# Making the triangular inverses of two DeltaNet heads together instead of one at a time

## The chip, the cores and the metric

The kernel runs on one core of one Trainium2 chip. The metric is device time of the whole program in microseconds (us). Before the change three runs took 2318.16, 2314.65 and 2317.48 us, a median of 2317.48 us. PE is the matrix engine (PEld its weight load), DVE, ACT and POOL are the vector, scalar and GpSimd engines, and SP is the queue that issues every DMA of this kernel.

## The reference, cut to what matters

One hybrid encoder layer over 2048 prompt positions and a 32-position sample, width 1024, all in 32-bit floats. A combined input projection feeds a spatial-gating mixer and a gated DeltaNet with 4 heads of 128; an output projection and a feed-forward of width 4096 follow. The change is inside the DeltaNet. For every head and chunk the reference solves a unit triangular system:

```
kb = k * beta[..., None]
a = jnp.einsum('bhnid,bhnjd->bhnij', kb, k) * dec_strict
lmat = a + jnp.eye(C, dtype=a.dtype)
rhs = jnp.concatenate([v * beta[..., None], kb * jnp.exp(gc)[..., None]], axis=-1)
sol = lax.linalg.triangular_solve(lmat, rhs, left_side=True, lower=True, unit_diagonal=True)
...
def step(s, inp):
    v_new = u_i - jnp.einsum('bhck,bhkv->bhcv', w_i, s)
    o = jnp.einsum('bhck,bhkv->bhcv', qg_i, s) + jnp.einsum('bhij,bhjv->bhiv', attn_i, v_new)
    s = s * gl_i[..., None, None] + jnp.einsum('bhck,bhcv->bhkv', kg_i, v_new)
```

The kernel works in chunks of 128 positions and forms the inverse of each 128x128 unit triangular matrix itself. There are 16 such chunks per head, in two halves of the sequence with 8 chunks each, and a small 32-position one for the sample.

## The kernel before, in words

The program records operations, each with an engine, an estimated duration, its operands and a priority, and a list scheduler (`schedule`, line 249) then writes them out in one order per engine. Each engine executes its list strictly in that order. Six priorities exist: CHAIN (the recurrence), INV (the inverses), LOCAL, EVAC, GEMM (the large projections) and IDLE. PE's list is mostly large matmuls of 260 to 512 columns (tiles `g`, `f`), with small bursts put between them when the scheduler's clock says that their operands are ready. On PE, `schedule` adds to an operation's cost 95 or 110 ns when the array's tile shape changes, and 84 ns (`TURN`) when a large matmul follows a small one.

The stages are: start-up; per half of the sequence `v_stage`, the q/k/v projections, the DeltaNet parts and `u_stage`; then `out_stage` for each half; then the feed-forward. The DeltaNet of one head and half has three parts.

- `delta_local` (LOCAL) forms, per pair of chunks, the decayed key products; they land in a buffer `nb` of 8 matrices of 128x128 (tile `M` of `delta_inv`).
- `delta_inv` (INV, line 1236) inverts the 8 matrices. The 16x16 diagonal blocks go by DMA to a layout with one block per partition (64 rows of 256 numbers), and `solve` (line 1298) inverts them on POOL with 15 pairs of multiply and subtract. They go back by DMA into `ud`. PE then doubles the size of the inverted blocks: from 16 to 32 with two bursts of 32 matmuls each on four 32x32 quarters of the array (`pa`, `pb`), from 32 to 64 with two bursts on 32x32 places (`p1` on two places, 16 matmuls; `p2` on three, 24 matmuls, the third making a transpose), and from 64 to 128 with two bursts of 8 matmuls on one 64x64 quarter (`p3`, `p4`). Each result is negated or copied by DVE before the next burst reads it. All use the one PSUM bank `B`.
- `delta_chain` (CHAIN, line 1411) runs over the chunks for heads 0 and 1 together, then 2 and 3, and needs both heads' inverses. Each chunk has three small bursts in banks `C`.

A 32-bit matmul of such a burst is two instructions in the trace, so 32 calls are 64 instructions there. `sample` does the same for the 32 sample positions, with its own solve on 8 rows. The chain's and the sample's outputs go through DRAM (`mix_d`) and are read back by `load_group` (line 943) into `BH`/`BL` for `out_stage`. The staging tiles of `load_group`, `x_stats`, `v_tile` and `gate_tile` come from the ring `E`, with six places of 512 columns before.

## Time and profile before

| what | value |
|---|---|
| median of the runs shown | 2317.48 us (2314.65 to 2318.16) |
| span of the profiled execution, first to last instruction | 2313.1 us |
| what the median has beyond that span | 4.4 us |
| PE busy | 2289.8 us, 99% |
| DVE, ACT, POOL busy | 1664.5, 1228.2, 602.1 us |

The page gives the profiled execution's own time as its span; the 4.4 us beside it are the difference to the median of other executions. Timeline rows give the start in us from the first instruction, the time from the first start to the last end of a merged group, the engine, the source line, the operation, the tiles (`out<-in`), the shapes and the number of instructions. `32*32 32x16` is a matmul on 32 rows and 32 columns of the array with 16 moving columns. Matmuls overlap in the pipeline, so what a group costs PE is read from the starts of the large matmuls on either side of it, not from its own length.

### The profile page before, as it was taken

To read this page: it belongs to the slowest core of one execution; us is meant where nothing else is said; L and a number is where in the kernel's file an instruction comes from. 1 tells how busy PE (TensorE), PEld (TensorE's weight loads), DVE (VectorE), ACT (ScalarE), POOL (GpSimd) and SP (SyncE) were. 2 spreads that over 40 slices of the span, in tenths; PEclk is the share of its full clock that TensorE was granted. 3 is DMA by queue.
4 is the path that set the end of the run, shared out by engine and by line. 5 is a ranking of instruction groups with operands and counts; after the bars stand their busy time and mean duration, and the time that the engine had idled before them with its cause. 6 is when DMAs were issued, how large, how long until landed. Compare 5 with 4: busy or idle time off the path is not lost.

```text
span 2313.1 us, 45814 instructions
## 1 busy us (share of the span) xinstructions
PE 2289.8 (99%) x16018; PEld 2178.3 (94%) x16018; DVE 1664.5 (72%) x3619; ACT 1228.2 (53%) x2809; POOL 602.1 (26%) x846
## 2 busy tenths in 40 slices
PE   9999999999999999999999999999999999999998
PEld 6887779999999988999999999999999999999998
DVE  6657656677654555589999999876668886666775
ACT  4665657566564434476555545753344564344344
POOL 1224443324333023444445424210000250000001
PEclk9999999999999999999999999999999999999999
DMA  8478876666566766887777787997667797766771
GB/s 314 147 253 297 258 227 221 186 203 209 169 200 187 244 203 217 265 295 256 257 252 262 254 282 241 336 327 237 216 215 257 257 305 231 223 215 217 250 223 54
DMA packets 358327, 547.08 MB, mean 237 GB/s; under 512 B 66424, under 2 KB 182284, under 8 KB 358096
## 3 DMA queue, kind: packets, MB, share of 16 engines
q1 hardware_dynamic: 358096, 544.16, 72.5%
q8 instruction: 126, 2.06, 0.4%
q14 instruction: 105, 0.86, 0.1%
HBM read 390.96 MB, written 153.05 MB: 235 GB/s over the span
## 4 chain that ended last, share of the span: by engine, by line
PE 65%; DVE 2%; DMA 1%; issue 1%; ACT 1%; POOL 0%; POOLq 0%; DVEq 0%; SPq 0%; ACTq 0%
PE f L416 53%; PE g L416 10%; PE C L416 1%; DMA s<-th_d 1%; DVE s L370 1%; POOL s L370 0%; DVE wl L370 0%; ACT s L355 0%; PE B L416 0%; DVE BL L370 0%; DMA x_d<-s 0%; PE C L427 0%; PE M L416 0%; PE M L427 0%; ACT BH L355 0%
## 5 line engine op out<-in xcount | busy, mean ns | idle before, releaser
L355 ACT ACTIVATE s<-s 128x348 f32<-128x348 f32 (+12 forms) x1067 | 490.7, 484 | 328.7 <-DVE s L370 144.4
L416 PE MATMUL f<-s,wh 128*128 128x348 f32 (+1 forms) x2768 | 662.0, 322 | 0.5 <-DVE s L370 0.3
L416 PEld LDWEIGHTS f<-s,wh 128*128 128x128 f32 x2768 | 481.0, 188 | 1.8 <-DVE s L370 1.4
L370 DVE TENSOR_TENSOR s<-f,s 128x348 f32<-128x348 f32 (+1 forms) x696 | 347.4, 511 | 168.2 <-PE f L416 167.5
L416 PE MATMUL f<-s,wl 128*128 128x348 f32 (+1 forms) x1384 | 444.7, 321 | 0.0
L416 PE MATMUL g<-BH,wh 128*128 128x384 f32 (+2 forms) x1088 | 399.5, 367 | 3.4 <-ACT BH L355 3.4
L416 PE MATMUL g<-BH,wl 128*128 128x384 f32 (+2 forms) x1088 | 382.3, 351 | 0.0
L416 PE MATMUL g<-BL,wh 128*128 128x384 f32 (+2 forms) x1088 | 381.2, 350 | 0.3 <-DVE BL L375 0.3
L370 DVE TENSOR_TENSOR s<-s,s 128x348 fp32r<-128x348 f32 (+8 forms) x674 | 347.1, 544 | 40.7 <-ACT s L355 16.9
L416 PE MATMUL f<-BL,wh 128*128 128x348 f32 (+1 forms) x1024 | 330.1, 322 | 0.0
L416 PE MATMUL f<-BH,wh 128*128 128x348 f32 (+1 forms) x1024 | 329.0, 321 | 0.0
L416 PE MATMUL f<-BH,wl 128*128 128x348 f32 (+1 forms) x1024 | 328.6, 321 | 0.0
L355 ACT ACTIVATE wh<-s 128x512 fp32r<-128x512 f32 x282 | 176.4, 632 | 234.7 <-PE f L416 178.7
L370 POOL TENSOR_TENSOR s<-s 64x15 f32<-64x15 f32 (+12 forms) x328 | 163.9, 500 | 447.3 <-issue 382.1
L370 POOL TENSOR_TENSOR s<-s,s 128x512 f32<-128x512 f32 (+5 forms) x153 | 186.3, 1225 | 308.2 <-ACT s L355 155.5
L416 PEld LDWEIGHTS f<-s,wl 128*128 128x128 f32 x1384 | 260.5, 188 | 0.0
L370 DVE TENSOR_TENSOR wl<-s,wh 128x512 fp32r<-128x512 f32 x282 | 221.4, 792 | 37.1 <-ACT wh L355 36.6
L416 PEld LDWEIGHTS g<-BH,wh 128*128 128x128 f32 x1088 | 205.0, 188 | 26.6 <-issue 4.9
L416 PEld LDWEIGHTS g<-BL,wh 128*128 128x128 f32 x1088 | 205.5, 189 | 17.2 <-DVE BL L375 0.9
L416 PEld LDWEIGHTS g<-BH,wl 128*128 128x128 f32 x1088 | 204.6, 188 | 18.2
L375 DVE SCALAR_TENSOR_TENSOR s<-s,s,s 128x256 f32<-128x256 f32 (+4 forms) x314 | 163.9, 547 | 53.7 <-ACT s L355 29.1
L416 PEld LDWEIGHTS f<-BH,wl 128*128 128x128 f32 x1024 | 192.6, 188 | 0.0
(133 smaller groups left out, 3350.0 us busy)
## 6 DMA issues: line engine op xcount, KB each, us to landing
s<-w_u SPq DMA_DIRECT2D x124, 256.0 KB, 4.0
s<-w_d SPq DMA_DIRECT2D x121, 256.0 KB, 3.4
wh<-su_d SPq DMA_DIRECT2D x114, 256.0 KB, 3.8
wl<-su_d SPq DMA_DIRECT2D x114, 256.0 KB, 3.9
wh<-sd_d SPq DMA_DIRECT2D x100, 256.0 KB, 3.1
wl<-sd_d SPq DMA_DIRECT2D x100, 256.0 KB, 3.9
wr<-w_b SPq DMA_DIRECT2D x36, 512.0 KB, 5.1
s<-adaw SPq DMA_DIRECT2D x32, 512.0 KB, 6.1
```

The costliest lines, as they stand in the source:

```text
L355: self.p.op(ACT, c, lambda: nc.scalar.activation(out=R(out), in_=R(in_), func=func, **{k: R(v) for k, v in kw.items()}), [out, accum], [in ...
L370: self.p.op(eng, c, lambda: e.tensor_tensor(out=R(out), in0=R(a), in1=R(b), op=op), [out], [a, b])
L375: self.p.op(DVE, c, lambda: nc.vector.scalar_tensor_tensor(out=R(out), in0=R(a), scalar=R(s), in1=R(b), op0=op0, op1=op1), [out], [a, s, b])
L416: nc.tensor.matmul(R(out), R(l), R(r), **kw)
```

## The change

The inverses are made for a pair of heads at once. `delta` now collects two `nb` buffers and calls `delta_inv` once for both. `solve` works on 128 rows instead of 64. Each burst of 16, 32 and 64 covers 16 chunks. The third place of `p2` is gone: the transpose that it made is now a DVE 32x32-block transpose. The step from 64 to 128 has three bursts instead of four for two heads: the upward products of the first head; then the downward products of the first head and the upward ones of the second, alternating, on two different quarters of the array; then the downward ones of the second. The scheduler no longer adds anything for a changed tile shape or for a turn to a large matmul, and the bursts have other durations in it. To make room, `nb` has three places instead of two, the ring `E` four instead of six, and `N`, `U`, `tmp`, `ud`, `td`, `z0`, `z1` lie elsewhere.

```diff
-TURN = 84
...
             if e == PE:
-                if o.table and o.table != grid:
-                    end += 110 if o.table == (P, P) else 95
-                    grid = o.table
-                elif o.prio == GEMM and not large:
-                    end += TURN
                 large = o.prio == GEMM
...
-        rg("nb", [(5, 0), (24, 0)], (P, 1024))
+        rg("nb", [(5, 0), (24, 0), (23, 0)], (P, 1024))
...
-        rg("E", hv(21, 22, 23), (P, 512))
+        rg("E", hv(21, 22), (P, 512))
...
-        with self.p.at(INV):
-            self.delta_inv(hf, h, nb)
+        self.nbs.append(nb)
+        if len(self.nbs) == 2:
+            with self.p.at(INV):
+                self.delta_inv(hf, h // 2, self.nbs)
+            self.nbs = []
...
-        Uv = self.solve(64, nd)
+        Uv = self.solve(128, nd)
...
-        at = [(c, a, slice(32 * a, 32 * a + 32)) for c in range(8) for a in range(4)]
+        C = range(16)
+        at = [(c, a, slice(32 * a, 32 * a + 32)) for c in C for a in range(4)]
-        self.mms([(pa[x, 16 * c : 16 * c + 16], M[x, c, x], td[x, c, 0:16], kw(32 * a, 32 * a)) for c, a, x in at], 480)
+        self.mms([(pa[x, 16 * c : 16 * c + 16], M(x, c, x), td[x, c, 0:16], kw(32 * a, 32 * a)) for c, a, x in at], 1396)
...
-        self.mms([(p1[hi[p], 32 * e : 32 * e + 32], M[lo[p], e, hi[p]], td[lo[p], e], kw(64 * p, 64 * p + 32))
-                  for e in range(8) for p in range(2)], 350)
+        self.mms([(p1[hi[p], 32 * c : 32 * c + 32], M(lo[p], c, hi[p]), td[lo[p], c], kw(64 * p, 64 * p + 32))
+                  for c in C for p in range(2)], 800)
...
-            calls.append((p2[32:64, 256 + 32 * e : 288 + 32 * e], ud[32:64, e], z1[32:64, e], kw(32, 32)))
-        self.mms(calls, 380)
-        self.cp(TA[32:64, :, 0:32], e8(p2[32:64, 256:512]))
+        self.mms([(p2[lo[p], 32 * c : 32 * c + 32], z1[hi[p], c], ud[hi[p], c], kw(64 * p + 32, 64 * p))
+                  for c in C for p in range(2)], 800)
+        self.transpose32(TA[32:64, :, 0:32], bl(p2[0:32, 0:512], 32))
...
-        self.mms([(p3[64:128, 64 * e : 64 * e + 64], M[0:64, e, 64:128], TA[:, e], kw(0, 64)) for e in range(8)], 880)
-        self.ts(z2[64:128], e8(p3[64:128, 0:512]), -1.0, ALU.mult)
-        p4 = self.bank("B")
-        self.mms([(p4[0:64, 64 * e : 64 * e + 64], z2[64:128, e], M[64:128, e, 64:128], kw(64, 0)) for e in range(8)], 880)
+        up = lambda c: (p3[64:128, 64 * (c % 8) : 64 * (c % 8) + 64], M(slice(0, 64), c, slice(64, 128)), TA[:, c], kw(0, 64))
+        dn = lambda c: (p3[0:64, 64 * (c % 8) : 64 * (c % 8) + 64], z2[64:128, c], M(slice(64, 128), c, slice(64, 128)), kw(64, 0))
+        self.mms([up(c) for c in range(8)], 1251)
+        self.ts(z2[64:128, heads[0]], bl(p3[64:128, 0:512], 64), -1.0, ALU.mult)
+        self.mms([f for c in range(8) for f in (dn(c), up(c + 8))], 1251)
+        self.ts(z2[64:128, heads[1]], bl(p3[64:128, 0:512], 64), -1.0, ALU.mult)
+        self.cp(Ms[0][0:64, :, 64:128], bl(p3[0:64, 0:512], 64))
+        self.dma(self.us_d[2 * pair][hf], nbs[0])
+        self.mms([dn(c) for c in range(8, 16)], 1251)
```

Where the instructions stand. The first place is PE's list at the step from 64 to 128 of the last head (before) and of the last two heads (after) of the second half. `B_...` is the PSUM bank of the inverses, `g_...` a bank of a large projection, `C_...` a bank of the chain; `s_...` are slots of SBUF. Before:

```order
L416 MATMUL g_9278<-BH_74,wl 128x384
L416 MATMUL B_9388<-s_477,s_491 64x64 x8
L416 MATMUL g_9278<-BH_75,wh 128x384
...
L416 MATMUL g_9278<-BH_78,wl 128x384
L416 MATMUL B_9427<-s_491,s_477 64x64 x8
L427 MATMUL C_9312<-ident,s_471 128x128 x2
```

and now:

```order
L410 MATMUL C_9255<-s_477,s_465 128x128 x4
L410 MATMUL B_9250<-s_473,s_468 64x64 x8
L410 MATMUL g_9140<-BH_77,wh 128x288
...
L410 MATMUL g_9241<-BH_75,wl 128x288
L410 MATMUL B_9250<-s_468,s_473 64x64
L410 MATMUL B_9250<-s_473,s_487 64x64
...
L410 MATMUL g_9241<-BH_76,wh 128x288
...
L410 MATMUL g_9307<-BH_74,wl 128x288
L410 MATMUL B_9250<-s_487,s_473 64x64 x8
```

Two bursts of 8 per head became three for two heads; the middle one alternates single matmuls whose weights are `s_468` and `s_473`, 16 in all. All three write the same bank.

The second place is PE's list at the end of the sample's chain: its last transpose (`C_...<-ident`), and behind it the first large matmul of `out_stage` for the second half (the first `128x384` after the `128x512`) and the first one that reads the sample's columns (`128x288`). Before:

```order
L416 MATMUL g_10486<-BH_73,wl 128x512
L427 MATMUL C_10469<-ident,s_473 128x128
L416 MATMUL g_10486<-BH_74,wh 128x512
...
L416 MATMUL g_10624<-BH_71,wh 128x384
...
L416 MATMUL g_10827<-BH_71,wh 128x288
```

and now:

```order
L410 MATMUL g_10303<-BH_71,wh 128x384
...
L410 MATMUL g_10404<-BH_75,wl 128x384
L421 MATMUL C_10375<-ident,s_469 128x128
L410 MATMUL M_10379<-ones,s_487 128x1 x4
L410 MATMUL g_10404<-BH_76,wh 128x384
...
L410 MATMUL g_10549<-BH_71,wh 128x288
```

Between the transpose and the first matmul on the sample's columns stood 159 large matmuls, and now stand 57: the transpose, with the chain ahead of it, has moved back by 102 large matmuls.

## The prediction

> **What bounds the kernel now.** I read the page first, then the busy times by stage, then PE's timeline around the bursts of the inverses. The page:

> ```profile
> span 2313.1 us, 45814 instructions
> PE 2289.8 (99%) x16018; PEld 2178.3 (94%) x16018; DVE 1664.5 (72%) x3619; ACT 1228.2 (53%) x2809; POOL 602.1 (26%) x846
> ```

> PE is idle for 23 us of 2313. The inverses lie between 300 and 770 us; the busy times of the two stretches that hold them (length; PE, PEld, DVE, ACT, POOL; clock; DMA) say the same of that place alone:

> ```profile
> 230.00:480.00 250.00, 247.88 (x2339) 216.67 (x2338) 161.25 (x490) 154.55 (x457) 91.13 (x199) 1.00 0.72 223
> 600.00:780.00 180.00, 179.39 (x1844) 172.14 (x1844) 102.29 (x318) 93.05 (x270) 64.30 (x178) 1.00 0.63 190
> ```

> There PE idles 2.1 of 250 us and 0.6 of 180 us, at full granted clock. So what an inverse does on DVE, ACT, POOL or by DMA is covered by large matmuls, and the time is PE's list added up. The change is worth what it takes from that list, less the new places where PE has to stand.

> **What a burst costs now.** In PE's timeline I take the start of the large matmul before a burst and of the second one after it, and subtract two ordinary pitches between large matmuls. Counting to the second one includes what the first pays to get back in.

> ```profile
> 635.84 0.29 PE L416 MATMUL g<-BH,wh 128*128 128x288 f32 x1
> 635.97 0.29 PE L416 MATMUL g<-BL,wh 128*128 128x288 f32 x1
> 636.10 0.29 PE L416 MATMUL g<-BH,wl 128*128 128x288 f32 x1
> 636.33 0.73 PE L416 MATMUL B<-s,s 32*32 32x16 f32 x64
> 636.98 0.40 PE L416 MATMUL g<-BH,wh 128*128 128x288 f32 x1
> 637.22 0.29 PE L416 MATMUL g<-BL,wh 128*128 128x288 f32 x1
> ...
> 596.40 0.29 PE L416 MATMUL g<-BH,wl 128*128 128x288 f32 x1
> 596.62 0.69 PE L416 MATMUL B<-s,s 32*32 32x32 f32 x32
> 597.24 0.40 PE L416 MATMUL g<-BH,wh 128*128 128x288 f32 x1
> 597.48 0.29 PE L416 MATMUL g<-BL,wh 128*128 128x288 f32 x1
> ...
> 470.54 0.34 PE L416 MATMUL g<-BL,wh 128*128 128x384 f32 x1
> 470.72 0.34 PE L416 MATMUL g<-BH,wl 128*128 128x384 f32 x1
> 470.99 0.70 PE L416 MATMUL B<-s,s 32*32 32x32 f32 x48
> 471.62 0.44 PE L416 MATMUL g<-BH,wh 128*128 128x384 f32 x1
> 471.89 0.33 PE L416 MATMUL g<-BL,wh 128*128 128x384 f32 x1
> ...
> 760.46 0.33 PE L416 MATMUL g<-BH,wl 128*128 128x384 f32 x1
> 760.72 1.14 PE L416 MATMUL B<-s,s 64*64 64x64 f32 x16
> 761.79 0.45 PE L416 MATMUL g<-BH,wh 128*128 128x384 f32 x1
> 762.08 0.34 PE L416 MATMUL g<-BL,wh 128*128 128x384 f32 x1
> ```

> The pitch is 0.13 us at 288 columns (635.84, 635.97, 636.10) and 0.18 at 384 (470.54, 470.72). A burst of 16 costs 637.22 - 636.10 - 0.26 = 0.86 us, the first burst of 32 costs 597.48 - 596.40 - 0.26 = 0.82, the second 471.89 - 470.72 - 0.36 = 0.81, a burst of 64 costs 762.08 - 760.46 - 0.36 = 1.26. A head has two, one, one and two of them: 1.72 + 0.82 + 0.81 + 2.52 = 5.87 us, and the 8 heads (4 in each half) 47.0 us.

> The same rows show what a burst is made of. The groups by form give the length of one instruction (number, busy us, mean ns, idle time before them):

> ```profile
> L416 PE MATMUL B<-s,s 64*64 64x64 f32 x256 | 18.2, 221 | 0.2 <-DVE s L393 0.2
> L416 PE MATMUL B<-s,s 32*32 32x16 f32 x1032 | 12.0, 180 | 0.4 <-DVE s L401 0.4
> L416 PE MATMUL B<-s,s 32*32 32x32 f32 x640 | 11.2, 192 | 0.0
> ```

> Bursts of 32, 48 and 64 instructions of the 32x32 forms last 0.69, 0.70 and 0.73 us, nearly the same, because they use two, three and four places of the array and each place gets 16. Less one instruction (0.19 or 0.18) that is 0.50, 0.51 and 0.55 us, or 0.031 to 0.034 us for a round in which every place takes one instruction. So different places run beside each other at no cost, all writing one PSUM bank. On a single 64x64 place the round takes (1.14 - 0.22) / 15 = 0.061 us. What is left of a burst's price, 0.86 - 0.55 = 0.31 or 0.82 - 0.50 = 0.32 us, is paid once per burst for entering and leaving.

> **The change part by part.** *Joint small bursts.* A joint burst has 32 rounds on each place where a single one had 16. It costs one more set of rounds and saves one entry: 0.86 + 0.55 = 1.41 for 16, 0.82 + 0.50 = 1.32 and 0.81 + 0.50 = 1.31 for 32 (the third place that p2 loses ran beside the others, so dropping it gives nothing). For a pair of heads 2 x 1.41 + 1.32 + 1.31 = 5.45 us, in place of 2 x 3.35 = 6.70: 1.25 saved.

> *The step of 64.* The outer bursts stay at 1.26. The middle one has 32 instructions on two quarters, with different rows and different columns. If they run beside each other as the 32x32 places do, it takes 16 rounds and half a round more: 1.26 + 0.03 = 1.29. If not, 16 further instructions at 0.061 come on top: 1.26 + 0.98 = 2.24. I take 1.29, since the nearest rows (two places with different rows and columns, 0.69 us for 32 instructions) behave so. Then a pair costs 1.26 + 1.29 + 1.26 = 3.81 in place of 5.04: 1.23 saved; with no overlap 0.28.

> *Sum.* 1.25 + 1.23 = 2.48 us per pair of heads; there are 4 pairs (two per half), so 9.9 us. Against the profiled span 2313.1 - 9.9 = 2303.2 us; the median of the runs has 4.4 us beyond that span, so 2307.6 us. With no overlap the saving is 4 x 1.53 = 6.1 us.

> *POOL.* A solve of 64 rows and the sample's of 8 rows, 30 instructions each:

> ```profile
> 671.83 11.43 POOL L370 TENSOR_TENSOR s<-s 64x15 f32<-64x15 f32 x30 [6.84 <-DMA s<-nd_d]
> 742.46 11.99 POOL L370 TENSOR_TENSOR s<-s 8x15 f32<-8x15 f32 x30 [5.00 <-DMA s<-nds_d]
> ```

> Eight rows take as long as 64, so 128 should too, and four solves (46 us) leave POOL. I count that at nothing: PE does not wait for POOL in this stretch. The smaller count of copies, table loads and DMAs is counted at nothing for the same reason; the large matmuls cover it.

> *The scheduler's durations.* No charge is left for a turn to large matmuls. PE's order stays a fixed list; a charge only moves a burst forward or back in it. Now 800 ns stand for bursts of 32 that cost about 1.3 us by the sum above. The scheduler's PE is then ahead of the real one, so more large matmuls than needed stand before the next step, which makes a wait on PE rarer. I count it at nothing.

> *The end of the chain.* The inverse of heads 2 and 3 now waits for both, and with it their chain and the sample's last transpose, which moves from the row at 888.68 to the place of the row at 912.47, 57 large matmuls before the row at 922.98. Its outputs must go to DRAM and back and be split before that.

> ```profile
> 888.68 0.27 PE L427 MATMUL C<-ident,s 128*128 128x128 f32 x1
> ...
> 912.47 0.34 PE L416 MATMUL g<-BH,wh 128*128 128x384 f32 x1
> ...
> 922.98 0.30 PE L416 MATMUL g<-BH,wh 128*128 128x288 f32 x1
> ...
> 888.99 0.35 DVE L375 SCALAR_TENSOR_TENSOR s<-C,s,s 128x128 f32<-128x128 f32 x1 [1.45 <-PE C L427]
> ...
> DMA to landing us min/median/max: 1.5/3.9/6.1
> ...
> 914.88 0.46 DVE L370 TENSOR_TENSOR BL<-s,BH 128x288 fp32r<-128x288 f32 x1 [0.29 <-ACT BH L355]
> ```

> The path is 0.31 + 0.35 to the end of the DVE step, two landings on mix_d of 3.9 at the median, and about 0.9 for the two halves of the split (0.46 each): 9.4 us, against 10.5. At the longest landings (6.1) it is 13.8, and PE would stand some 3 us, with the loads behind it in SP's queue late by as much. I take none and keep 3 for the range. The ring E with four places instead of six hits the same loads: a wave of four takes a landing and a split, about 5 us, so the 8 tiles of a group take 10 us, while 48 large matmuls at 0.18 us, 8.6 us, stand between two groups in PE's list. Two groups short by 1.4 us give 0 to 3 us more.

> [...]

> **The rivals.** [...]

> *New waits eat part of it*: the late end of the chain and the four places of E, 2 to 6 us together. For it: the margin of 1.1 us above. Against it: the short waits of today. It gives 2309.6 to 2313.6, in the middle 2311.6 us. This is also the case in which the pairs do not pay as meant, because an inverse that waits for two heads is later.

> *The chain's steps come too late in PE's list*: slower. The other durations reshuffle all dependent bursts, and where PE arrives before the operand it stands, with every large matmul queued behind. There are 96 chain bursts (2 halves x 2 pairs x 8 chunks x 3) and 28 of the inverses. It decides from a mean wait of 0.12 us on each of the 124 on: 14.9 us, 2307.6 + 14.9 = 2322.5 us. Today's waits speak against it, 0.6 and 0.4 us in total:

> ```profile
> PE C L416 <- ACT s L355: 0.6, 1, 0.6
> PE B L416 <- DVE s L401: 0.4, 1, 0.4
> ```

> *More than the sum*: two of today's waits of PE on ACT between large matmuls, 3.1 us, could happen to vanish with fewer table loads. It gives 2304.5 us.

> **How the numbers follow.** The full sum, with waits within 2 us of today's, has 0.57; no overlap 0.10; new waits 0.20; late chain steps 0.07; more than the sum 0.06. The predicted time is that of the first, 2307.6 us. The range reaches down to 2303.5, a little below the last case, and up to 2314.5, past the first three cases; it leaves out the late chain steps and the ends of the others. I call a change of over 0.2% (4.6 us, so below 2312.8 or above 2322.1) one that a measurement of this kernel can tell. Faster then has nearly all of the first, second and last cases and about half of the third, lowered for what a reshuffled list can hide: 0.79. Within 0.2% gets 0.14 and slower 0.07.

> **What would show it.** In the changed kernel's timeline a burst of 128 instructions of the form 32x16 should last about 1.28 us, one of 64 of the form 32x32 about 1.2, and the middle burst of 32 of the form 64x64 about 1.17 us; 2.1 us there means no overlap. PE's busy time should fall by some 9 us with its idle time near 23 us. POOL should fall by about 46 us, and a solve should stay near 11 to 12 us. The prediction is wrong if PE's idle time grows by more than 3 us; the places to look are the chain's bursts after 700 us and the loads of mix_d before 923 us.

## The result, and the profile after

The changed kernel takes 2321.86 us (median of 6 runs, 2320.62 to 2328.52), the kernel before took 2317.14 us beside it (6 runs, 2314.62 to 2318.16). The ratio is 1.0031 with a 95% interval of 1.0021 to 1.0041: slower, by about 7 us by the ratio (the two medians differ by 4.7 us), where 9.9 us of gain were forecast. The profiled execution has a span of 2320.9 us (before 2313.1).

The page of the changed kernel, span and engine line:

```profile
span 2320.9 us, 45340 instructions
PE 2289.5 (99%) x15890; PEld 2180.3 (94%) x15890; DVE 1651.0 (71%) x3591; ACT 1215.4 (52%) x2794; POOL 568.1 (24%) x722
```

POOL fell by 34 us, but PE's busy time did not fall. The same two stretches as in the prediction, with the columns named there:

```profile
230.00:480.00 250.00, 243.32 (x2144) 215.87 (x2144) 150.83 (x443) 146.34 (x435) 77.96 (x142) 0.97 0.69 215
600.00:780.00 180.00, 177.38 (x1883) 172.65 (x1882) 96.13 (x303) 90.13 (x270) 55.32 (x151) 0.99 0.62 186
```

PE now idles 6.7 us of the first stretch (before 2.1) and 2.6 us of the second (before 0.6), and the granted clock, 1.00 before, is 0.97 and 0.99. What PE waits for (total us, times, longest):

```profile
PE B L410 <- issue: 6.7, 4, 2.2
PE f L410 <- DVE s L364: 2.7, 4, 1.1
PE C L410 <- DMA s<-us_d: 2.3, 1, 2.3
```

The first line is new. "Issue" means that PE stood although nothing that the profile shows held it. PE's timeline around the first pair's two joint steps of 16 shows where:

```profile
340.22 0.40 PE L410 MATMUL g<-BH,wl 128*128 128x512 f32 x1
340.54 1.26 PE L410 MATMUL B<-s,s 32*32 32x16 f32 x128
...
344.19 0.61 PE L410 MATMUL B<-s,s 32*32 32x16 f32 x50
346.97 0.84 PE L410 MATMUL B<-s,s 32*32 32x16 f32 x78 [2.17 <-issue]
```

The first joint burst lasts 1.26 us (1.28 was forecast). The second one stops after 50 of its 128 matmuls for 2.17 us, in the middle of a list of calls that are all ready. All four pairs do so; the other three stops are 1.92, 1.80 and 0.82 us long.

The next view is the busy time, the granted clock and the DMA share in four short stretches behind such stops (columns as above):

```profile
348.76:352.17 3.41, 3.41 (x10) 2.65 (x9) 0.28 (x1) 3.37 (x10) 0.00 (x0) 0.50 0.23 39
386.31:389.72 3.41, 3.41 (x18) 3.41 (x17) 3.26 (x12) 2.94 (x7) 0.00 (x0) 0.50 0.47 155
464.81:471.64 6.83, 6.83 (x26) 6.54 (x25) 3.13 (x8) 4.35 (x12) 0.00 (x0) 0.50 0.42 118
645.72:649.13 3.41, 3.41 (x62) 3.01 (x62) 2.08 (x6) 1.51 (x6) 0.18 (x1) 0.50 0.12 41
```

PE counts as busy through all 17.06 us of them, at half the clock. About half of that time is lost (8.5 us by the clock, 7.9 us against the median pitch of the same forms), and no line of waits shows it. In the kernel before, the trace has no such stretch between 20 and 2300 us. Three of the four follow the stops of 1.80 to 2.17 us in the bursts. The one at 386.31 follows a wait of the first pair's chain for the inverse's output:

```profile
383.15 0.38 PE L410 MATMUL C<-s,s 128*128 128x128 f32 x2
385.88 0.49 PE L410 MATMUL C<-s,s 128*128 128x128 f32 x2 [2.35 <-DMA s<-us_d]
386.12 0.41 PE L410 MATMUL g<-wh,BH 128*128 128x260 f32 x1
386.33 0.42 PE L410 MATMUL g<-wl,BH 128*128 128x260 f32 x1
```

The pitch of the large matmuls of 260 columns behind it is 0.21 us (386.12 to 386.33); a few us earlier, between 378 and 381 us, it is 0.12 us.

The bursts that do not stop cost what was forecast. The timeline shows the middle step of 64 and a joint step of 32:

```profile
786.24 0.29 PE L410 MATMUL g<-BH,wl 128*128 128x288 f32 x1
786.46 1.15 PE L410 MATMUL B<-s,s 64*64 64x64 f32 x32
787.54 0.40 PE L410 MATMUL g<-BH,wh 128*128 128x288 f32 x1
...
771.88 1.20 PE L410 MATMUL B<-s,s 32*32 32x32 f32 x64
```

32 instructions on two quarters last 1.15 us (1.17 forecast), as long as 16 on one (1.14). So the two 64x64 quarters do run beside each other although both write one PSUM bank. POOL's joint solve of 128 rows also costs what was forecast:

```profile
730.53 11.00 POOL L364 TENSOR_TENSOR s<-s,s 128x15 f32<-128x15 f32 x30 [4.60 <-DMA s<-nd_d]
```

**A ledger of PE's time.** For the experiments I add up each trace in one way. The time from one PE instruction's start to the next is work up to the median of that form. What goes more than 0.3 us beyond the median is a wait, and what is lost in the stretches at half clock stands apart. Steps in the small bursts up to 0.5 us over count as work. "Mixers" ends where the feed-forward part's first large matmul starts. All numbers are differences to the profiled execution before, in us:

| kernel | work in the mixers | waits | half clock | sum of mixers | feed-forward part | sum |
|---|---|---|---|---|---|---|
| changed kernel | -10.6 | +7.8 | +7.1 | +4.4 | +3.5 | +7.9 |
| e1, spaced 5 us | -8.5 | +8.1 | +3.5 | +3.1 | +1.1 | +4.2 |
| e5, hybrid | -9.7 | +5.2 | 0.0 | -4.4 | +3.1 | -1.3 |
| e6, only the 64s joint | -5.6 | +4.3 | +0.2 | -1.0 | +3.7 | +2.7 |
| e9, before with less work | -9.4 | 0.0 | +1.5 | -7.9 | +2.9 | -5.0 |
| e10, changed, half a first step | -13.4 | +8.0 | +3.7 | -1.7 | +4.0 | +2.3 |
| e13, 16s split | -7.6 | +6.5 | +4.1 | +3.1 | +0.1 | +3.2 |
| e14, before reordered | -0.2 | -1.6 | 0.0 | -1.8 | +2.1 | +0.3 |

The three columns of one kernel depend on how the median is taken: by pairs of neighbouring forms over all traces, the changed kernel has -11.4, +6.0 and +9.7, with the same sum of 4.4. So a single column is good to some 3 us, the sums to 0.1 us. The forecast's 9.9 us of work are there: 10.6. They were paid back as 7.8 us of waits (6.7 of them the four stops), 7.1 us of half clock, and 3.5 us in the feed-forward part.

### The profile page after: what moved, and what is told of

It reads as the page before. It is cut to its first block, busy times and chain, and to the rows that moved or that the text cites. A ratio compares the mean times of both kernels' runs of the same rounds, so it can differ in the third digit from the quotient of the medians.

```text
span 2320.9 us, 45340 instructions
## 1 busy us (share of the span) xinstructions
PE 2289.5 (99%) x15890; PEld 2180.3 (94%) x15890; DVE 1651.0 (71%) x3591; ACT 1215.4 (52%) x2794; POOL 568.1 (24%) x722
## 4 chain that ended last, share of the span: by engine, by line
PE 92%; DVE 3%; ACT 2%; issue 1%; DMA 1%; POOL 0%; SPq 0%; POOLq 0%; DVEq 0%; ACTq 0%
PE f L410 53%; PE g L410 29%; PE C L410 3%; PE B L410 2%; PE L L410 2%; DVE s L364 2%; PE M L410 1%; PE L L421 1%; ACT s L349 1%; DVE s L369 0%; ACT L349 0%; DVE wl L364 0%; SPq L402 0%; DMA wr<-w_b 0%; ACT wh L349 0%
## 5 line engine op out<-in xcount | busy, mean ns | idle before, releaser
L349 ACT ACTIVATE s<-s 128x348 fp32r<-128x348 f32 (+13 forms) x1059 | 488.3, 487 | 331.9 <-DVE s L364 135.6
L364 DVE TENSOR_TENSOR s<-s,s 128x348 fp32r<-128x348 f32 (+6 forms) x674 | 350.6, 548 | 42.0 <-ACT s L349 18.1
L364 POOL TENSOR_TENSOR s<-s,s 128x512 f32<-128x512 f32 (+15 forms) x303 | 239.1, 792 | 358.2 <-ACT s L349 131.7
L364 DVE TENSOR_TENSOR wl<-s,wh 128x512 fp32r<-128x512 f32 x282 | 213.3, 764 | 41.4 <-ACT wh L349 41.1
L410 PEld LDWEIGHTS g<-BH,wl 128*128 128x128 f32 x1088 | 205.6, 189 | 18.3
L410 PEld LDWEIGHTS f<-BH,wh 128*128 128x128 f32 x1024 | 192.4, 188 | 2.1 <-ACT wh L349 1.3
L410 PEld LDWEIGHTS f<-BL,wh 128*128 128x128 f32 x1024 | 192.3, 188 | 0.4 <-DVE BL L364 0.3
```

Of the source, the lines that this page charges most:

```text
L349: self.p.op(ACT, c, lambda: nc.scalar.activation(out=R(out), in_=R(in_), func=func, **{k: R(v) for k, v in kw.items()}), [out, accum], [in ...
L364: self.p.op(eng, c, lambda: e.tensor_tensor(out=R(out), in0=R(a), in1=R(b), op=op), [out], [a, b])
L410: nc.tensor.matmul(R(out), R(l), R(r), **kw)
```

## The experiments

**Where the stops lie.** This needs no run. I counted PE's records (matmuls and weight loads) from the start of the trace to the first instruction behind a stop. Stops inside a burst of 16 of over 0.5 us from start to start, in all kernels that have them:

| kernel | stops (us) at records | record modulo 256 |
|---|---|---|
| changed | 4290, 6849, 9921, 12225 | 194, 193, 193, 193 |
| e1, e2 | 12481; 4290 | 193; 194 |
| e7 | 6593, 8129, 11713 | 193, 193, 193 |
| e8 | 4290, 6849, 9921, 12225 | 194, 193, 193, 193 |
| e10, e13 | 4290, 6593; 4290, 6850 | 194, 193; 194, 194 |

All 17 lie at the same place of a grid of 256. The trace's DMA queue 8, of kind "instruction", moves 125 packets of 16384 bytes in the whole run, one per 256 records of PE (32109 in all), or 64 bytes per instruction. The DMA view of 343.5 to 346.9 us, around the first stop (packets, MB, share of 16 engines):

```profile
q1 hardware_dynamic: 840, 1.31, 103.7%
q8 instruction: 1, 0.02, 1.6%
```

In the trace of the changed kernel the four packets that matter start 2.2 to 2.7 us before PE goes on (for instance 461.93 and 464.16 us). I read it so: PE had run to the end of what was fetched, and the next block came late. That the 840 packets of data held it back is likely, but not shown: no run takes the data away. In all traces together, the 94 packets that start over 2 us behind the block boundary before them stand where the data queue is busy 90% of the time (median of the 4 us around that boundary), the others where it is busy 73%.

The same count tells the boundaries with a stop from the others. The 18 traces have 2209 such boundaries, the first three of each left out, and each has its packet (both counted from the start). Where the packet started 2.9 us or more before PE got to the boundary, the step over it never took more than 0.35 us. In the other 34 it started less than 2.8 us before, and all 17 stops are among them; PE then went on 2.2 to 2.7 us after the packet's start. The shortest lead in the kernel before is 3.0 us. How fast PE runs a block does not tell them apart: from boundary to boundary the block ahead of the four stops of the changed kernel took 3.7 to 6.1 us, the stop included, and the kernel before ran blocks in 3.5 and 4.8 us without a stop. Two stops of this kind stand outside the bursts of 16: one of 0.72 us in e10 between large matmuls (644.92 us), and one in e3, the old kernel with a shorter ring, in single bursts (459.85 us). The latter in e3's list of waits:

```profile
PE M L416 <- issue: 1.1, 1, 1.1
```

**e1 and e2: room between the two steps of 16.** After the first step's negation the scheduler is told of 5000 or 2000 ns more latency.

```diff
 self.ts(z0[:, :, 0:16], s16(pa[:, 0:256]), -1.0, ALU.mult)
+self.p.ops[-1].lat = 5000.0        # e2: 2000.0
```

> The changed kernel, with one number of the list scheduler altered: 5000 ns more between the negation of the first joint burst of 16 and the second burst, so that more large matmuls stand between the two; same instructions. Theory S (instruction supply): two bursts of 256 PE instructions (weight loads and matmuls) within 3 to 4 us use up the fetched instructions; PE stands about 2 us in the second burst, and the clock is halved for 3.4 or 6.8 us behind it. With more than 8 us between them the waits put down to issue on B (6.7 us, 4 times) fall under 0.5 us, the half-clock stretches between 50 and 800 us fall from 17 us to under 4, and the time is 2306 to 2312 us. Rival D (the joint burst itself is too dense for the array or its bank): the second burst stops for about 2 us wherever it stands; 2319 to 2324 us. Rival R (the reshuffled lists and the shorter ring E cost the time): the stops may go, the time stays over 2317 us.

> The same with 2000 ns. Theory S: about 5.5 us between the bursts, near the time that a fetch takes (3.8 to 6 us from use to use): the four stops fall to 0 to 1 us each, 2308 to 2317 us, between the changed kernel and the run with 5000 ns. Rival D: four stops of about 2 us, 2319 to 2324 us. Rival R: over 2317 us.

e1 took 2319.63 us, ratio 1.0025 (1.0015 to 1.0034); e2 2317.51 us, 1.0016 (1.0007 to 1.0025). The profiled execution of e2 is its slowest (2325.27 us), with 4.4 us of waits for a DMA near 184 us that no other trace has. The waits on issue in bursts fell from 6.7 us to 1.0 and 0.8 us. Most of the gain did not come, and e1's trace shows why in part. At the large matmul behind the last transpose of the kernel before, e1 is 9.5 us ahead (879.20 against 888.71 us). But 71 small matmuls of the chain, done by then in the kernel before, still lie ahead of e1 there; they are worth 5.5 us by the medians of their forms, so its true lead is 4.0 us. What is missing before that place are waits for ACT and DVE of 0.9 to 2.5 us (382, 427, 493 and 753 us), 6.83 us at half clock behind the one at 493.32, and the stop that is left. Some 48 us later e1 is 1.0 us behind (927.17 against 926.16 us). In e1's timeline, the end of the sample (C is its last transpose) and what waits for it; rows of PE, ACT and SP's queue are picked, others stand between them:

```profile
919.60 0.27 PE L421 MATMUL C<-ident,s 128*128 128x128 f32 x1
919.63 0.42 PE L410 MATMUL g<-BH,wh 128*128 128x384 f32 x1
919.89 0.34 PE L410 MATMUL g<-BL,wh 128*128 128x384 f32 x1
920.07 0.34 PE L410 MATMUL g<-BH,wl 128*128 128x384 f32 x1
920.24 0.29 PE L410 MATMUL g<-BH,wh 128*128 128x288 f32 x1
920.29 1.75 SPq L402 DMA_DIRECT2D mix_d<-s  x4
923.51 1.87 SPq L402 DMA_DIRECT2D s<-mix_d  x4
926.67 0.80 ACT L349 ACTIVATE BH<-s 128x288 fp32r<-128x288 f32 x2 [4.64 <-DMA s<-mix_d]
927.17 0.40 PE L410 MATMUL g<-BH,wh 128*128 128x288 f32 x1 [3.58 <-ACT BH L349]
```

Before the change this transpose ran at 888.68 us. The joint inverse of the last pair ends 26 us later than two single ones (its last burst starts at 790.53 instead of 764.11 us), and from that burst to the transpose it takes 129 us here and 125 us before, so the chain does not make the lateness up. In e1's list only 3 large matmuls stand between the transpose and the first `128x288` (919.63 to 920.07), where the changed kernel has 57 and the kernel before 159. The 24 matmuls from there on run before the loads of `mix_d` have landed, so they read other tiles; the next one waits 3.58 us for the chain's outputs, and PE gets half clock for 3.41 us behind it. e2, also with 3 large matmuls there, waits 3.68 us at 932.18. This wait belongs to the spaced lists. The changed kernel has none at this place, and neither has e10 (below), which has its list and passes the place 6 us earlier (921.30 against 927.36 us).

**e3 and e4: two side parts of the change alone**, made in the kernel before: four places of E instead of six; and the scheduler without its charges.

```diff
-rg("E", hv(21, 22, 23), (P, 512))
+rg("E", hv(21, 22), (P, 512))
```

```diff
-if o.table and o.table != grid:
-    end += 110 if o.table == (P, P) else 95
-    grid = o.table
-elif o.prio == GEMM and not large:
-    end += TURN
```

> The kernel before, with the ring E of four places instead of six and nothing else. Theory S: E is not what costs the time; 2315 to 2320 us. Rival R: E is behind it; over 2321 us.

> The kernel before, without the scheduler's charges for a turn (84 ns) and for a changed tile shape (95 and 110 ns) and nothing else. Theory S: only the order moves a little; 2313 to 2320 us. Rival R: the reshuffled lists cost the time; over 2321 us.

e3: 2316.23 us, ratio 1.0010 (1.0001 to 1.0019). e4: 2312.87 us, 0.9992 (0.9983 to 1.0001). Neither explains 7 us.

From here on the expectations name theories by letters: S, the instruction fetch and the clock behind its stops; L, the late end of the joint inverse; O, any new order costs time; J, the joint form does; P, PE's work counts in full while the order stands; G, it is given back; C, the missing charges make the plan too hopeful.

**e5: the last pair head by head, the others joint and spaced.** The single form is the old one on the new tiles; only its middle step of 64 is overlapped with the other head's.

```diff
+if hf == 1 and h > 1:
+    self.delta_head(hf, h // 2, h % 2, nb)     # solve and bursts of one head
-if len(self.nbs) == 2:
+elif len(self.nbs) == 2:
     self.delta_inv(hf, h // 2, self.nbs)       # with e1's 5000 ns
```

> Three pairs are inverted together as in the spaced kernel (5000 ns between the two steps of 16); the last pair (second half, heads 2 and 3) is solved and inverted head by head, and only its middle steps of 64 overlap. Theory L (the joint inverse delivers the last pair some 22 us later than two single ones, so the token-by-token sample and what follows it have no cover left at the end of the mixers): the sample's four stores into mix_d, at 920.3 us in the spaced kernel, come before 905 us; the wait of PE on BH of 3.6 us near 923 and the half clock behind it go; time = 2319.6 - 3.75 - 1.7 + 1.3 (the last pair now saves 1.2 instead of 2.5) = about 2315.5. Theory O (any new order of the instructions costs some us, wherever the inverses end): 2319 to 2321, with other waits of the same sum.

2314.03 us, ratio 0.9996 (0.9987 to 1.0005), against 1.0025 for e1: some 6 us better, where theory L expected 4. The sample's four stores that start at 920.29 us in e1 start at 899.85, the wait on BH is gone, and no half clock is left between 20 and 1400 us. The mixers are 4.4 us shorter than before the change. Part of that is luck: e5 still has e1's wait for ACT (2.49 us at 495.44), but without the 6.83 us at half clock behind it.

**e6 and e12: everything head by head, only the middle steps of 64 joint**, without and with the scheduler's old charges.

```diff
+# second head of a pair; the first head has made up(0) alone
+self.mms([f for g in zip(dn(M0, y0), up) for f in g], 1251)
+self.mms(dn(M, z2), 1251)
```

> All eight heads are solved and inverted head by head in single bursts as before the change, and only the second step of 64 of a pair's first head is put together with the first step of 64 of its second head, call by call, on two quarters of the array. Four bursts of 64 fewer: saving 4 x 1.2 = 4.9 us of PE. Theory S (the loss comes from bursts of 512 small matmuls and loads within 4 us, which the instruction fetch cannot feed, and from the half clock after each stop): no stop marked issue over 0.8 us inside a burst, no half clock between 50 and 900 us. Theory L: the last pair's inverse ends as early as before the change, so no wait on BH near 923. Both: before - 4.9 = about 2310, or 2311.7 if the start has 6.8 instead of 3.4 us at half clock. Theory O: 2316 to 2320.

> Head by head with only the middle steps of 64 overlapped, as in the run of that form before, and the scheduler's old charges (95, 110 and 84 ns) put back. Saving of PE work 4.9 us. Theory C (the plan without charges is too hopeful): the waits of 5 us between 384 and 398 us go, 2315.5 - 4.9 = about 2310.5, ratio 0.997 to 0.999. Rival (the waits come from the new places of the inverses, whatever the charges): 2315 to 2319 as without them.

e6: 2318.43 us, ratio 1.0020 (1.0007 to 1.0033). There is no stop over 0.5 us in a burst and no half clock in the mixers behind the start, as theory S asks, but the 5 us of work are eaten by waits at the start of the first pair's chain, where the changed kernel waits for us_d. PE's rows of e6 with idle time before them there:

```profile
385.46 0.73 PE L410 MATMUL B<-s,s 32*32 32x16 f32 x64 [0.79 <-DVE s L378]
389.71 0.55 PE L421 MATMUL L<-ident,s 128*128 128x128 f32 x3 [2.05 <-DVE s L369]
394.31 1.16 PE L410 MATMUL C<-s,s 128*128 128x128 f32 x8 [0.64 <-DVE s L369]
399.83 0.38 PE L410 MATMUL C<-s,s 128*128 128x128 f32 x1 [1.58 <-DVE s L369]
```

e12 took 2324.69 us, ratio 1.0037 (1.0025 to 1.0050). In its trace the waits between 384 and 400 us are gone (none over 0.5 us), as theory C asks, but others stand elsewhere (1.39 us at 342.60, 1.33 at 501.66, 1.37 at 699.96), and the time did not fall. The charges did not help: theory C falls here.

**e7: the old kernel with long bursts.** Each call of the steps of 16 is made twice; the order of all else is that of the kernel before.

```diff
-kw(32 * a, 32 * a)) for c, a, x in at], 480)
+kw(32 * a, 32 * a)) for c, a, x in at for _ in range(2)], 480)   # both steps
```

> The kernel before the change, its order untouched, with every call of the two steps of 16 made twice (the second writes the same numbers to the same place), so that each of the 16 single bursts is 128 matmuls long as in the joint form. Work added: 16 x 64 x 0.0085 = 8.7 us. Theory S: the fetch falls behind here too: in half or more of the eight second bursts a stop of 0.8 to 2.2 us, each at the same instruction number modulo 256, and half clock of 3.4 or 6.8 us after those over 1.8 us; time before + 8.7 + 8 to 28 = 2332 to 2352. Rival (the stop belongs to the joint form: one bank, two tiles of two heads, or a late z0): no stop, before + 8.7 = about 2324.

2334.83 us in a single run, beside 2315.93 us (median) of the kernel before: 18.9 us for 8.7 us of work. Its waits on issue, and the second burst of one head:

```profile
PE B L416 <- issue: 4.5, 3, 2.2
```

```profile
418.96 0.46 PE L416 MATMUL B<-s,s 32*32 32x16 f32 x28
421.20 0.99 PE L416 MATMUL B<-s,s 32*32 32x16 f32 x59 [1.78 <-issue]
```

Half clock followed for 6.83 and 3.41 us (421.11, 472.31 us). Work, stops and half of the 10.24 us at half clock make 8.7 + 4.5 + 5.1 = 18.3 us. So neither the joint form nor its tiles make the stops: long bursts in the old kernel do it too, though in three of the eight second bursts, and only two of these over 0.8 us, where half or more of the eight were expected.

**e8: the middle step of 64 in sequence.**

```diff
-self.mms([f for c in range(8) for f in (dn(c), up(c + 8))], 1251)
+self.mms([dn(c) for c in range(8)] + [up(c + 8) for c in range(8)], 1251)
```

> The changed kernel with the middle step of 64 not alternated: the eight calls of the first head's second step, then the eight of the second head's first step; order of all else untouched. If two quarters of the array run at once only when neighbours in the queue name different quarters, this burst takes 0.92 + 0.93 = 1.85 us from first to last start instead of 0.93, four times: the time is after + 3.7 = about 2325.6. If the overlap does not come from the alternation (or the 0.93 is something else), 0.93 stays and the time is that of the changed kernel, 2321.9.

One run, 2320.84 us. The burst, in e8's timeline:

```profile
368.24 1.90 PE L410 MATMUL B<-s,s 64*64 64x64 f32 x32
```

1.90 us instead of 1.15: the overlap of the quarters is worth 0.75 us per pair and comes from the alternation. The time did not rise by it, because in this execution the stops were shorter (3.7 us in all). The same boundary has stops of 2.17 us in one trace and 0.50 us in the other, so one run cannot carry a difference of 3 us.

**e9: as much work taken from the kernel before, its order untouched.**

```diff
-... for e in range(8)], 880)            # both steps of 64
+... for e in range(4)], 880)
-... for c, a, x in at], 480)            # the first step of 16
+... for c, a, x in at[:16]], 480)
```

> The kernel before the change with its order untouched and less work on PE: the single bursts of the two steps of 64 and of the first step of 16 make only half of their calls (half of each inverse is left out, so the output is not the reference's). Work taken away: 16 x 8 x 0.058 + 8 x 32 x 0.0085 = 7.4 + 2.2 = 9.6 us, about the 9.9 us that the change was to save. Theory P (PE sets the time of the mixers: what its bursts lose in length the kernel gains, as long as the order of all instructions stands): 2315.5 - 9.6 = about 2306, ratio 0.9958. Theory G (the saving is given back, because loads, DVE, ACT or the chain set the time of the mixers as soon as PE is 10 us faster): 2311 to 2315, ratio over 0.998, with waits of PE some 6 us above those of the kernel before.

2306.63 us, ratio 0.9965 (0.9953 to 0.9978): 8.9 us gained by 9.6 us of work. Theory P holds, G falls. In its page PE's busy time falls by 6.3 us:

```profile
span 2308.2 us, 45045 instructions
PE 2283.5 (99%) x15634; PEld 2170.2 (94%) x15634; DVE 1658.3 (72%) x3619; ACT 1226.7 (53%) x2809; POOL 601.4 (26%) x846
```

So what the forecast said of the bound was right: without new waits, PE's work counts nearly in full.

**e10: the changed kernel with half a first step**, order untouched (the first step of 16 is made for the pair's first head only, so the second head's inverse is left incomplete).

```diff
-kw(32 * a, 32 * a)) for c, a, x in at], 1396)      # first step of 16
+kw(32 * a, 32 * a)) for c, a, x in at[:32]], 1396)
```

> The changed kernel with its order untouched, whose first joint step of 16 makes only the calls of the pair's first head (64 instead of 128 matmuls; the second head's inverse is left wrong). From the first of the two steps to the end of the second there are then some 404 matmuls and loads instead of 532. Work taken away: 4 x 0.54 = 2.2 us. Theory S (the fetch of instructions falls behind only in that density): no stop marked issue in the second step, none of the four half-clock stretches behind it: 2321.9 - 2.2 - 6.7 - 6.8 = about 2306; if then PE reaches the end of the mixers so early that it waits for the sample's mix_d as in the spaced kernel (theory L), 3.8 + 1.7 more, 2311.5. Rival (the stop belongs to the second joint step itself): stops of 0.8 to 2.2 us stay, about 2319.5.

2318.10 us, ratio 1.0013 (1.0003 to 1.0022). This is far from the 2306 and 2311.5 us of theory S, and near the 2319.5 us of its rival, the second joint step itself. Yet two of the four stops in the second steps went, which the rival does not give, and two stayed, one longer than any before:

```profile
457.60 1.08 PE L410 MATMUL B<-s,s 32*32 32x16 f32 x107
462.18 0.51 PE L410 MATMUL B<-s,s 32*32 32x16 f32 x21 [3.50 <-issue]
```

All four second steps still hold a block boundary. In the two that stopped the packet started 2.2 and 2.4 us before PE went on (342.74 and 459.79 us), the second of them 5.3 us after the boundary before it; in the other two it had started 2.9 and 8.7 us before PE reached the boundary (755.69 and 632.35 us). The number of instructions in the pair of steps is therefore not the criterion, as I had put it. The stops go with how long before the boundary the packet starts, as the count over all traces has it (under 2.8 us at all 17); that a fast burst only shortens this time is my reading.

**e11: the hybrid with the old charges**, the diff of e4 reversed on e5.

> The hybrid (three pairs together and spaced, the last pair head by head) with the list scheduler's old charges put back: 95 and 110 ns for a turn between shapes of the array and 84 ns for a large matmul behind a small one. Theory C (the plan without these charges is too hopeful, so DVE and ACT work is planned late and PE waits some 5 us more in the mixers and 3 us more in the feed-forward part): 2314 - 4 to 8 = 2306 to 2310, ratio 0.996 to 0.998. Rival (the charges are worth nothing, the waits come with any order of joint inverses): 2312 to 2316.

2313.56 us, ratio 0.9992 (0.9984 to 1.0001); the hybrid without them had 0.9996. No difference that can be told: the charges were rightly counted at nothing.

**e13: joint solve and steps of 32 and 64, the steps of 16 head by head**, the last pair as in e5, no added wait. Unlike what was expected of it, this kernel has the scheduler's old charges: it is e11 with the steps of 16 split and the 5000 ns taken out.

```diff
+for e in range(2):
+    pa = self.bank("B")
+    self.mms([... for c, a, x in at if c // 8 == e], 860)
+    ...
+    pb = self.bank("B")
+    self.mms([... for c, a, x in at if c // 8 == e], 860)
```

> Three pairs with one joint solve and joint steps of 32 and 64, but the two steps of 16 made head by head, each head's first and second after the other, with no added wait; the last pair head by head as in the hybrid; no charges in the scheduler. Saving of PE work 3 x 1.8 + 1.2 = 6.6 us. Theory S (a block of 256 instructions of PE that is run in under some 3 to 5 us outruns its fetch): these bursts are as dense as those before the change, so no stop over 0.8 us marked issue and no half clock between 50 and 900 us. With theory P (a saving counts in full where no wait is added): 2315.5 - 6.6 = 2309, ratio 0.9972; with the 3 to 5 us of other waits that all reordered forms showed, 2312 to 2314. If stops appear, the form of the bursts and not their density makes them: 2316 or more.

2320.41 us, ratio 1.0023 (1.0014 to 1.0032). That is some 7 us more than e11. It was meant to be free of stops and had two, 2.7 us together:

```profile
461.49 0.59 PE L415 MATMUL B<-s,s 32*32 32x16 f32 x49
464.09 0.31 PE L415 MATMUL B<-s,s 32*32 32x16 f32 x15 [2.00 <-issue]
```

So bursts of 64 matmuls one behind the other, with few large ones between them, stop at block boundaries as well (records 4290 and 6850). It also waits 2.4 us for us_d at the place where the changed kernel does.

**e14 to e16: the old kernel in other orders.** One number of the scheduler is moved.

```diff
-SLACK = 400
+SLACK = 380        # e15: 420; e16: TURN = 90 instead of 84
```

> The kernel before the change with one number of the list scheduler moved, 380 ns instead of 400 of slack for the results of small matmuls; every instruction is the same, some stand in another order. Theory O (any new order of this length of program brings its own waits, several us either way, and those of the reordered forms are of that kind): this run and its two companions spread over 2312 to 2322, with at least one of them 3 us or more from 2315.5. Theory J (the waits come from the joint form: later inverses, fewer and longer bursts): all three within 2 us of the kernel before.

> As its companion, with 420 ns instead of 400. Theory O: spread over 2312 to 2322. Theory J: within 2 us of the kernel before.

> As its companions, with the charge for a large matmul behind a small one at 90 ns instead of 84. Theory O: spread over 2312 to 2322. Theory J: within 2 us of the kernel before.

2315.32, 2315.97 and 2314.32 us, ratios 1.0004 (0.9994 to 1.0013), 1.0000 (0.9990 to 1.0009) and 0.9998 (0.9989 to 1.0008). These three orders cost nothing that can be told, so theory O falls as it was put. That the waits of 4 to 8 us belong to the reordered forms themselves is what is left, but three small shifts of the old list do not prove it.

## Why the prediction was wrong

- *What bounds the kernel*: right. e9 gains 8.9 us by 9.6 us less work in the same order.
- *The burst prices, 1.41, 1.32, 1.31 and 1.29 us, and the sum of 9.9 us*: right as work (10.6 us in the ledger). The failing step is the first of them. "A joint burst ... costs one more set of rounds and saves one entry" was taken from the kernel before, whose packets start 3.0 us or more ahead of their boundary. It did not hold where a packet came later. The second joint step of 16 took 2.1 to 3.5 us from first to last start, instead of about 1.1, because PE stood at a block boundary whose packet had started 0.1 to 1.7 us before. That is 6.7 us over four pairs.
- *Nothing in the prediction had the clock*, the second step that failed. It read "full granted clock" as a property of the kernel and put no term for it. 17 us at half clock followed the stops and one wait; the ledger has 7.1 us more loss than before.
- *No overlap of the quarters*: rejected by the 1.15 us and by e8. *More than the sum*: did not occur.
- *The end of the chain, 0 to 3 us, "I take none"*: right for the changed kernel, which has no wait there, and neither has e10 6 us earlier. The margin was larger than the 10.5 us of the sum: the first matmul that needs the chain's outputs stands 24 behind the row at 922.98, at 926.16 us. In e1 and e2, whose lists leave 3 large matmuls instead of 57, PE waits 3.58 and 3.68 us, and half clock follows, which the term did not have.
- *New waits eat part of it* was the right family, 2 to 6 us; the changed kernel shows one of 2.35 us at the start of the first pair's chain, which the prediction did not name. *The chain's steps come too late* came out at the right time (2322.5 against 2321.9 us) by a wrong mechanism, and so by luck: the chain's bursts wait at most 4.1 us in all, 0.04 us each instead of 0.12.
- *The scheduler's durations, E's four places and POOL, each counted at nothing*: borne out by e4, e11 and e3 within about 2 us, and by the solve of 11.00 us. POOL fell by 34 us and not 46; this cost nothing.
- *What would show it wrong* was named, in part: PE's idle time rose from 23 to 31 us (over 3 us). The places named were not where it happened, at 344 to 347, 462 to 464 and 643 to 646 us; only the fourth stop, near 764 us, is behind 700 us, and it is in an inverse, not in the chain.

Still open is the feed-forward part. Three profiles in the changed kernel's order (the changed kernel itself, e8, e10) are 3.5 to 4.0 us longer there than the one before, but e9, in the old order, is 2.9 us longer too. The waits at 384 to 400 us of e6 are seen, not isolated; with the charges (e12) they stand elsewhere. What delays a packet is open too. No version beat both kernels beyond its interval; e5 and e11 equal the old one.

## What to carry to other kernels

Price a burst of many tiny matmuls not only by the array but by instructions: count matmuls and loads per 256, the block in these traces, and ask whether the next block can arrive in time: here PE stopped at the start of a block only where the packet had started under 2.8 us before it was needed (34 of 2209 boundaries, with all 17 stops of the bursts among them). Look at the clock column behind every place with some 1.5 us of idle PE within 3.4 us, since the loss there can equal the idle time (here 3.41 us at clock 0.50, 1.7 us lost, behind 1.48 us or more of idle time in 17 of 19 cases) and stands in no list of waits. Before two dependent jobs are joined, look for what starts when the earlier one ends: here an inverse 26 us later left 57 of 159 large matmuls as cover at the other end of the stage, and a further delay (e1) used them up.
